# First two input projections accumulated tile by tile beside the modulation, and the steps of all stages placed one by one

## The chip, the cores and the metric

The kernel runs on one core of one Trainium2 chip. The metric is device time in microseconds (us); the median of three runs of the kernel before is 1701.49. TensorE is called PE here, VectorE DVE, ScalarE ACT, GpSimd POOL and SyncE SP, as in the profile. SP issues the transfers (DMAs); PE's results land in PSUM, from where DVE and ACT fetch them.

## The reference

One inference step of a transformer layer, on a batch of 1024 prompt frames and 64 sample frames, width D = 1024, all in fp32:

```python
mod = silu(c) @ w_ada + b_ada                       # 6 x 1024 shifts, scales, gates
h = rms_norm(x, norm1_g) * (1 + sc1) + sh1
proj = h @ w_in                                     # 3336 columns
...                                                 # columns 0-1791: RWKV-7 heads (8 x 64)
z = p_rwkv + (prev - p_rwkv) * shift_mu
r, k, v, dw, da, dg = split(z)
y_rwkv, s_new = rwkv_scan(...)                      # s = s*w + sa (kk a) + v k, y = s r
...                                                 # the rest: forgetting attention (8 x 64)
y_fox = softmax(q k^T / 8 + forget bias, causal) @ v
x = x + gt1 * (concat(y_rwkv, y_fox) @ w_out)
h2 = rms_norm(x, norm2_g) * (1 + sc2) + sh2
x = x + gt2 * ((silu(h2 @ w_ffn_gate) * (h2 @ w_ffn_up)) @ w_ffn_down)
```

Beside the output the step returns the RWKV state, the shifted row, and keys, values and log forget values.

## The kernel before

**Numbers.** Every large product is made of three matmuls: operands are split in a high part in a rounded format and a low part that holds the rest (`split_w`, L285: the cast whi on ACT, L212, the subtraction wlo on DVE, L216), and hi x hi, hi x lo and lo x hi are summed in PSUM (`mm3`, L291; lines L294, L295, L296). A weight tile of w_in is 1024 x 128 numbers, 512 KB; whi and wlo each have two buffers. One projection of a half of the tokens is 8 feature tiles x 3 = 24 matmuls.

**Tokens** go in two halves: half 0 has 512 columns, half 1 has 512 and the 64 sample frames, in two chunks of 288. Functions write the steps down in an order, a scheduler turns this into the order of the instructions on each engine.

**Start.** Modulation tile t of w_ada (16 of 48 are made here, in the order shift 0, scale 0, shift 1, scale 1, ...) takes 8 matmuls of 32x128 (`ada_mm`, L181, tile pada; the trace counts 16 records), a copy of the row by ACT (mrow, L193), a transpose on PE (L198) and on DVE a sum and an addition (mred, L200; mod, L201). After each pair DVE makes a gain (g, L204), and `h_part` makes feature tile k of the normed input: x on DVE (L270), its high part hhi on ACT (L271), its low part hlo on DVE (L272). SP loads the input, twelve modulation tiles, w_in tile 12, four modulation tiles, w_in tile 13. The splits of both come late, at tiles 12 and 15. Then come the projections of tiles 12 and 13 (for the low-rank gates), from PSUM buffers "mm".

**Phase.** Each half follows a string of steps (`ORDER`, L35; `phase`, L1286): Z (three projections k, r, v of one pair of RWKV heads), D, A, B, N (decay, triangular blocks, the recurrence, norm and output), Q, K, V (projections for the attention), q, k (norms), L, O, C, S, P (smaller steps). A round of modulation tiles left over (24, the "background") comes one ahead of each projection that loads a weight. Rows of B that the prediction speaks of: small 32x32 products pg (L523), one PSUM buffer for each head of the pair, tags rb and ch. What half 0 leaves undone is done later (T, U).

**Attentions.** Half 0 has 2 units per head, half 1 has 3, each of them in three parts: scores psc (L910, L912) with maximum and exponential, transposes ppt (L940) with splits pth and ptl, products with the values pav (L962). `Pipe(2)` runs each unit's first part two units ahead of its last. Between them half 1 has `residual_x`, `load_mix` (L984: tiles mixt of the mixed heads back from memory, split in mixrh, mixrl for the RWKV part, mixfh, mixfl for the attention part) and `outproj` of half 0 (matmuls po, 24 per output tile, O0 to O7), one output tile after each head. Between the two attentions PSUM buffers are laid out anew: first scores of half 1 need those of half 0 released.

**End.** Output projection of half 1, second norm, the feed-forward network and its down projection.

## Time and profile before

| | |
|---|---|
| median of three runs | 1701.49 us (1700.19 to 1702.09) |
| the profiled execution | 1699.15 us, its span 1697.5 us |
| ACT busy, DVE busy | 726.5 us (43%), 1124.8 us (66%) |
| bytes moved | 207.08 MB, mean 122 GB/s |
| mean granted clock of PE | 0.992 |

The profile covers one execution; times count from the span's start. A group's mean duration can mix shapes. PE's matmuls overlap in their records, so a matmul's cost in a row of them is the distance between two starts, not its duration. The granted clock is the share of full speed that PE was given.

### The profile page before, as it was taken

What the parts mean: (1) busy time and instruction counts of PE and PEld (TensorE: products, weight loads), DVE (VectorE), ACT (ScalarE), POOL (GpSimd) and SP (SyncE); (2) the same over time, 40 slices, a digit from 0 to 9 for tenths busy, and PEclk for the clock granted to TensorE, in tenths of its full rate; (3) what the DMA queues carried; (4) which work ended last, traced back from release to release, by engine and by line L of the source; (5) the groups of instructions that cost most, each with busy time, mean ns of one, the idle gap of its engine ahead of it and who ended that gap; (6) DMA issues with size and microseconds to landing.
All of it is one profiled execution on the core that took longest, in us unless ns stands there. A gap on an engine that the chain in (4) does not pass through costs nothing.

```text
span 1697.5 us, 33265 instructions
## 1 busy us (share of the span) xinstructions
PE 1645.3 (97%) x12897; PEld 1439.1 (85%) x12897; DVE 1124.8 (66%) x2573; ACT 726.5 (43%) x1530; POOL 183.1 (11%) x412
## 2 busy tenths in 40 slices
PE   6999999999999999989999999999999999999999
PEld 3776776788888888767889899999999999999998
DVE  6776676757867655877877975555555556545545
ACT  4535364653545346766776633333333333211210
POOL 2102230222121213201120000000000000000000
PEclk9999999999999999989999999999999999999999
DMA  8544447541233344566654432222222215323313
GB/s 308 164 128 133 141 135 200 176 123 33 71 85 85 87 135 113 149 190 179 169 181 167 157 127 77 77 77 77 77 77 77 77 65 196 134 79 97 97 40 121
DMA packets 133580, 207.08 MB, mean 122 GB/s; under 512 B 62126, under 2 KB 70350, under 8 KB 133422
## 3 DMA queue, kind: packets, MB, share of 16 engines
q1 hardware_dynamic: 133422, 204.95, 39.5%
q8 instruction: 102, 1.67, 0.4%
q14 instruction: 56, 0.46, 0.1%
HBM read 157.65 MB, written 47.25 MB: 121 GB/s over the span
## 4 chain that ended last, share of the span: by engine, by line
PE 84%; DVE 6%; ACT 4%; DMA 3%; issue 2%; SPq 0%; POOL 0%; ACTq 0%; DVEq 0%; POOLq 0%
PE pd L1275 15%; PE pfe L1160 8%; PE pfc L1160 7%; PE pfa L1160 7%; PE pmm L294 5%; PE pmm L295 5%; PE pmm L296 5%; PE pfb L1160 4%; PE pbs L375 2%; PE pav L962 2%; PE po L294 2%; PE ppt L940 2%; PE po L296 2%; PE po L295 2%; PE pA L464 2%
## 5 line engine op out<-in xcount | busy, mean ns | idle before, releaser
L294 PE MATMUL pmm<-hhi,whi 128*128 128x288 f32 (+1 forms) x624 | 218.8, 351 | 2.3 <-ACT pb L317 1.4
L295 PE MATMUL pmm<-hlo,whi 128*128 128x288 f32 (+1 forms) x624 | 217.0, 348 | 0.0
L296 PE MATMUL pmm<-hhi,wlo 128*128 128x288 f32 (+1 forms) x624 | 215.2, 345 | 0.6 <-DVE wlo L216 0.6
L212 ACT CAST whi<-wraw 128x1024 fp32r<-128x1024 f32 (+2 forms) x116 | 99.2, 855 | 212.5 <-PE pd L1275 167.0
L1275 PE MATMUL pd<-ah,wlo 128*128 128x512 f32 (+1 forms) x528 | 173.5, 329 | 0.0
L1275 PE MATMUL pd<-al,whi 128*128 128x512 f32 (+1 forms) x528 | 173.3, 328 | 0.0
L1275 PE MATMUL pd<-ah,whi 128*128 128x512 f32 (+1 forms) x528 | 173.1, 328 | 0.0
L1279 DVE SCALAR_TENSOR_TENSOR x1t<-pd,mod,x1t 128x512 f32<-128x512 f32 x192 | 91.4, 498 | 111.5 <-PE pd L1275 111.0
L294 PEld LDWEIGHTS pmm<-hhi,whi 128*128 128x128 f32 x624 | 119.0, 191 | 14.1 <-ACT pb L317 2.0
L296 PEld LDWEIGHTS pmm<-hhi,wlo 128*128 128x128 f32 x624 | 118.7, 190 | 10.9 <-issue 1.7
L295 PEld LDWEIGHTS pmm<-hlo,whi 128*128 128x128 f32 x624 | 118.7, 190 | 9.9 <-issue 1.2
L216 DVE TENSOR_TENSOR wlo<-wraw,whi 128x1024 fp32r<-128x1024 f32 (+2 forms) x108 | 104.2, 965 | 18.8 <-ACT whi L212 18.3
L1275 PEld LDWEIGHTS pd<-al,whi 128*128 128x128 f32 x528 | 99.4, 188 | 7.7
L1275 PEld LDWEIGHTS pd<-ah,whi 128*128 128x128 f32 x528 | 99.3, 188 | 7.7
L1275 PEld LDWEIGHTS pd<-ah,wlo 128*128 128x128 f32 x528 | 99.3, 188 | 7.5
L1160 PE MATMUL pfc<-hh,hS 128*128 128x256 f32 (+1 forms) x352 | 101.6, 289 | 1.6 <-ACT hh L1062 1.6
L1160 PE MATMUL pfc<-hl,hS 128*128 128x256 f32 (+1 forms) x352 | 101.9, 289 | 0.0
L1160 PE MATMUL pfa<-hh,whi 128*128 128x256 f32 (+1 forms) x352 | 101.9, 290 | 0.0
L1160 PE MATMUL pfa<-hl,whi 128*128 128x256 f32 (+1 forms) x352 | 101.8, 289 | 0.0
L1160 PE MATMUL pfc<-hh,lS 128*128 128x256 f32 (+1 forms) x352 | 101.5, 288 | 0.0
L1160 PE MATMUL pfa<-hh,wlo 128*128 128x256 f32 (+1 forms) x352 | 101.4, 289 | 0.0
L604 POOL TENSOR_SCALAR sd<-sv,pc 64x64 f32<-64x64 f32 x136 | 76.3, 561 | 181.2 <-DVE sv L617 157.6
(361 smaller groups left out, 4383.5 us busy)
## 6 DMA issues: line engine op xcount, KB each, us to landing
wraw<-in_w_in_dram SPq DMA_DIRECT2D x52, 512.0 KB
wada<-in_w_ada_dram SPq DMA_DIRECT2D x48, 512.0 KB
as<-actscr SPq DMA_DIRECT2D x22, 544.0 KB
wraw<-in_w_gate_dram SPq DMA_DIRECT2D x22, 512.0 KB
wraw<-in_w_up_dram SPq DMA_DIRECT2D x22, 512.0 KB
wraw<-in_w_down_dram SPq DMA_DIRECT2D x40, 256.0 KB
wraw<-in_w_out_dram SPq DMA_DIRECT2D x16, 512.0 KB
actscr<-sg SPq DMA_DIRECT2D x22, 288.0 KB
```

The costliest lines, as they stand in the source:

```text
L212: nc.scalar.copy(hi, src)
L216: eng.tensor_tensor(lo, src, hi.bitcast(F32), op=ALU.subtract)
L294: nc.tensor.matmul(ps[0:M, 0:n], whi[:, k, 0:M], xhi[:, k, off:off + n], start=(k == 0), stop=False)
L295: nc.tensor.matmul(ps[0:M, 0:n], whi[:, k, 0:M], xlo[:, k, off:off + n], start=False, stop=False)
L296: nc.tensor.matmul(ps[0:M, 0:n], wlo[:, k, 0:M], xhi[:, k, off:off + n], start=False, stop=(k == kt - 1))
L375: nc.tensor.matmul(ps[:, 0:n], w, x[:, off:off + n], start=True, stop=True)
L464: nc.tensor.matmul(pa[h][:, i], kb[hp, c + i], rk[hp, c + i], start=True, stop=True)
L604: nc.gpsimd.tensor_scalar(sd[hsl[h]], sv[hsl[h], c, h], pc[hsl[h], c], None, op0=ALU.mult)
L940: nc.tensor.transpose(pt[0:rows, b - b0, t * P:t * P + qn], p[0:qn, pc:pc + rows], self.ident[0:qn, 0:qn])
L1160: nc.tensor.matmul(ps, l[:, k], r[:, s, k], start=(first and k == 0 and y == 0), stop=(k == 3 and y == 2), skip_group_check=True)
L1275: nc.tensor.matmul(ps[:, 0:n], w[:, i], x[:, t:t + n], start=(i == 0 and y == 0), stop=(i == len(fs) - 1 and y == 2))
L1279: nc.vector.scalar_tensor_tensor(dst, ps[:, so - off:so - off + l], self.mod[:, 40 + o, b:b + 1], dst, op0=ALU.mult, op1=ALU.add)
```

## The change

No instruction is added or taken away; orders change in three places.

**Start.** The raw loads of w_in tiles 12 and 13 move up, behind modulation tiles 2 and 4; both splits stand ahead of the first feature tile. Two PSUM buffers are opened as sums, and after each feature tile its six matmuls (three per projection) are written down; `proj` then hands out the finished sums.

**Phases.** Z becomes X (k), Y (r) and W (v), each a step of its own, G is a background modulation tile given in the order, and A, B and T are generators, run in 3 or in 12 to 14 steps ("B0*12" runs twelve).

**Attentions.** `Pipe` goes; a string `ATT` gives every part of each unit, as a unit's number (0 stands for unit 0, each mention runs its next part), H for a head's loads, M and N for `load_mix` of half 0 and 1, R for `residual_x`, O for an output tile.

```diff
-ORDER = ("Z0 D0 A0 D1 Z1 L Q0 B0 V0 N0 A1 C0 Z2 D2 q0 O A2 K0 k0 B1 K1 V2 Z3 D3 Q1 q1 V1 C1 A3 S k1 Q2 N1 q2 Q3 B2 N2 K2 k2 V3 K3 k3 C2 q3 C3",
+ORDER = ("W0 X0 G Y0 G D0 A0*2 G D1 G X1 G Y1 A0 G W1 L G Q0 B0*12 G V0 N0 A1*3 C0 G X2 G Y2 G W2 D2 q0 A2 O A2*2 G K0 "
+         "k0 B1*12 G K1 G V2 G X3 G Y3 G W3 D3 G Q1 q1 G V1 C1 A3*3 S k1 G Q2 N1 B2 q2 G Q3 B2*11 N2 G K2 k2 G V3 G K3 "
...
+       "M H0 0 1 0 R 2 1 0 H1 3 2 1 4 3 2 5 4 3 O0 H2 6 5 4 7 6 5 8 6 7 O1 H3 9 8 7 10 9 8 11 10 9 O2 H4 12 11 10 13 "
...
     def proj(self, hf, col, evac):
+        if self.begun:
+            evac(self.begun.pop(0), 0, hf.n)
+            return
         if self.pre:
             whi, wlo = self.pre.pop(0)
         else:
-            if self.background:
-                self.background.pop(0)()
             whi, wlo = self.load_w(self.A["w_in"][col // P], [P, KT, P])
...
+    def att_phase(self, hf, order, more):
+
+        units = {}
+        for t in order:
+            if t[0] == "H":
+                us = self.attend(int(t[1:]), hf)
+                units.update({int(t[1:]) * len(us) + i: u for i, u in enumerate(us)})
+            elif t.isdigit():
+                next(units[int(t)], None)
+            else:
+                more[t[0]](int(t[1:] or 0))
...
                 for t in range(16):
-                    if t == 12:
-                        w_in(12)
+                    if t in (2, 4):
+                        w_in(11 + t // 2)
                     raw.append(self.ada_load(tile(t), "ada"))
-                w_in(13)
                 rs = self.x_stat(x0)
                 part = self.ada_mm(0, raw[0], "ra")
+                ws = [self.split_w(r, [P, KT, P]) for r in w]
+                self.begun = [self.ps([P, 512], tag="mm", name="pmm") for _ in w]
...
                     with tc.issue_after(part[4].ins):
-                        if t in (12, 15):
-                            self.pre.append(self.split_w(w.pop(0), [P, KT, P]))
                         if t and t % 2 == 0:
-                            self.h_part(hf, t // 2 - 1, x0[:, t // 2 - 1], rs)
+                            k = t // 2 - 1
+                            self.h_part(hf, k, x0[:, k], rs)
+                            for i, (whi, wlo) in enumerate(ws):
+                                for y, (a, b) in enumerate(((whi, self.hhi), (whi, self.hlo), (wlo, self.hhi))):
+                                    nc.tensor.matmul(self.begun[i], a[:, k], b[:, k, 0:512], start=(k == 0 and y == 0),
+                                                     stop=(k == KT - 1 and y == 2))
```

Line numbers in rows of the kernel after are its own, 12 to 34 higher than those before (L202 is the modulation matmul, L210 its transpose, L306 to L308 the three matmuls of a projection, L1466 those of the first two).

PE at the start, before: the last modulation tile, both last transposes, and then the first projection.

```order
L190 MATMUL pada<-wada,ct 32x128 x8
L198 MATMUL pada<-ident,mrow 128x128 x2
L294 MATMUL pmm<-hhi,whi 128x512
L295 MATMUL pmm<-hlo,whi 128x512
L296 MATMUL pmm<-hhi,wlo 128x512
```

PE at the start, after: one turn, the matmuls of feature tile 3 inside modulation tile 11 (its eight matmuls are cut in 1 and 7) and the two transposes behind it.

```order
L1466 MATMUL pmm<-hhi,whi 128x512 x2
L202 MATMUL pada<-wada,ct 32x128
L1466 MATMUL pmm<-hlo,whi 128x512
L1466 MATMUL pmm<-hhi,wlo 128x512
L1466 MATMUL pmm<-hlo,whi 128x512
L1466 MATMUL pmm<-hhi,wlo 128x512
L202 MATMUL pada<-wada,ct 32x128 x7
L210 MATMUL pada<-ident,mrow 128x128
L202 MATMUL pada<-wada,ct 32x128 x8
L210 MATMUL pada<-ident,mrow 128x128
```

The projections' matmuls moved from behind all modulation into it, and both transposes stand behind the matmuls that read hlo.

DVE in one turn of the same place, before:

```order
L200 TENSOR_REDUCE mred<-pada 128x2
L201 TENSOR_SCALAR mod<-mred,vc 128x2
L272 SCALAR_TENSOR_TENSOR hlo<-x_189,mod,hhi 128x512
L200 TENSOR_REDUCE mred<-pada 128x2
L201 TENSOR_SCALAR mod<-mred,vc 128x2
L204 SCALAR_TENSOR_TENSOR g_161<-mod,vc 128x2
L270 SCALAR_TENSOR_TENSOR x_189<-x_189,g_161,xacc 128x512
```

DVE in one turn, after:

```order
L212 TENSOR_REDUCE mred<-pada 128x2
L213 TENSOR_SCALAR mod<-mred,vc 128x2
L212 TENSOR_REDUCE mred<-pada 128x2
L284 SCALAR_TENSOR_TENSOR hlo<-x_189,mod,hhi 128x512
L213 TENSOR_SCALAR mod<-mred,vc 128x2
L216 SCALAR_TENSOR_TENSOR g_161<-mod,vc 128x2
L282 SCALAR_TENSOR_TENSOR x_189<-x_189,g_161,xacc 128x512
```

The second sum (mred), which needs the second transpose, moved ahead of hlo.

PE in half 0 at step B2, before: behind a projection (its last row here is pbs) and a background tile come products of both heads, pg_3365 for one and pg_3364 for the other, and then the next projection.

```order
L375 MATMUL pbs<-gsq,bmean 128x512
L190 MATMUL pada<-wada,ct 32x128 x8
L523 MATMUL pg_3365<-gt,At 32x32 x7
L368 MATMUL plora<-z,wg 128x512
L198 MATMUL pada<-ident,mrow 128x128
L523 MATMUL pw_3401<-g_3363,inv_692 32x32 x8
L523 MATMUL pu_3421<-inv_692,g_3363 32x32 x16
L523 MATMUL pg_3364<-gt,At 32x32 x16
L294 MATMUL pmm<-hhi,whi 128x512
```

The same place after (pgt and pu_3479 are later products of the first head):

```order
L388 MATMUL pbs<-gsq,bmean 128x512
L202 MATMUL pada<-wada,ct 32x128 x8
L540 MATMUL pw_3401<-g_3363,inv_742 32x32 x8
L540 MATMUL pu_3421<-inv_742,g_3363 32x32 x3
L381 MATMUL plora<-z,wg 128x512
L210 MATMUL pada<-ident,mrow 128x128
L540 MATMUL pu_3421<-inv_742,g_3363 32x32 x13
L540 MATMUL pgt<-gt,At 32x32 x8
L567 MATMUL pu_3479<-inv_742,gt 32x32 x8
L306 MATMUL pmm<-hhi,whi 128x512
```

The pg of the first head stand ahead of all this now, and pg_3364 come behind the projection that begins in the last row.

PE at the seam of the attentions, before: the last products of half 0 and the first scores of half 1.

```order
L962 MATMUL pav<-pth,vsx_8034 128x256
L962 MATMUL pav<-ptl,vsx_8034 128x256
L910 MATMUL psc<-k1x_9559,qsx_9557 128x512
L912 MATMUL psc<-k2x_9560,q2x_9558 128x512
```

PE at the seam, after (mixrh_9540 and mixrl_9544 are half 0's mixed RWKV heads):

```order
L306 MATMUL po<-mixrh_9540,whi 128x512
L307 MATMUL po<-mixrl_9544,whi 128x512
L984 MATMUL pav<-pth,vsx_8034 128x256
L962 MATMUL ppt<-ident,p 128x128
L308 MATMUL po<-mixrh_9540,wlo 128x512
L984 MATMUL pav<-ptl,vsx_8034 128x256
L306 MATMUL po<-mixrh_9540,whi 128x512
L984 MATMUL pav<-pth,vsx_8034 128x256
L962 MATMUL ppt<-ident,p 128x128 x2
```

SP at the seam, after, where the first load of a mix tile stands among the last loads for half 0:

```order
L895 DMA q2x_9558<-qx 64x576
L1018 DMA mixt<-yscr_71 128x512
L668 DMA yscr_72<-y 128x576
L901 DMA vsx_8034<-vscr_110 128x512
L996 DMA yscr_71<-fy 128x512
L1018 DMA mixt<-yscr_71 128x512
```

Matmuls of O0 moved from the first head of half 1 into the drain of half 0, twelve of them ahead of the first score, and the mix loads moved ahead of a store and of the last head's values.

146 lines of the change are left out of this document (72 added, 74 removed), and 3 rows, old and new, of the table ATT.

## The prediction

> **What bounds the kernel now.** I read the page first, then busy time by stretches, then the chain of waits at the places where a stretch had idle TensorE. The page's engine row:
>
> ```profile
> PE 1645.3 (97%) x12897; PEld 1439.1 (85%) x12897; DVE 1124.8 (66%) x2573; ACT 726.5 (43%) x1530; POOL 183.1 (11%) x412
> ```
>
> PE is busy 1645.3 of a span of 1697.5 us, so 52.2 us are idle, and the change keeps every PE instruction. What an order can win is idle time, and time at half clock. The stretches (length, then busy time of PE, PEld, DVE, ACT, POOL, then granted clock, DMA share, GB/s):
>
> ```profile
> 18.00:31.40 13.40, 9.28 (x187) 5.52 (x186) 10.95 (x34) 5.02 (x15) 6.32 (x21) 1.00 1.03 409
> 31.40:38.20 6.80, 6.13 (x42) 4.00 (x43) 6.07 (x20) 4.52 (x9) 0.00 (x0) 0.50 0.72 230
> 665.00:738.00 73.00, 65.56 (x522) 50.61 (x521) 58.91 (x190) 53.54 (x166) 17.92 (x56) 0.98 0.55 160
> 738.00:741.40 3.40, 2.25 (x12) 1.53 (x12) 2.53 (x8) 2.32 (x7) 0.15 (x2) 1.00 0.75 283
> 741.40:755.00 13.60, 11.98 (x40) 8.99 (x39) 7.17 (x14) 5.70 (x12) 0.41 (x2) 0.50 0.71 207
> 755.00:769.30 14.30, 13.06 (x76) 10.06 (x77) 10.62 (x24) 9.79 (x23) 0.35 (x2) 1.00 0.42 130
> 804.00:892.00 88.00, 87.98 (x540) 72.02 (x540) 70.54 (x145) 63.75 (x141) 18.43 (x27) 1.00 0.58 169
> 985.00:1431.00 446.00, 445.69 (x3545) 445.45 (x3544) 269.48 (x515) 138.31 (x256) 0.00 (x0) 1.00 0.26 85
> ```
>
> The reader should see two things. From 804 on PE is as good as full (87.98 of 88, later 445.69 of 446), so what is saved or lost before 804 reaches the end undiminished. And the open places are the start, where the first norm is made, and the seam between the two attentions at 738 to 769, where 1.15 + 1.62 + 1.24 = 4.0 us are idle and 11.98 us of PE work ran at a clock of 0.50, which is 6.0 us more than at full clock.
>
> **The start, part by part.** Before, the norm's loop goes round once per feature tile on DVE and ACT. The chain of waits:
>
> ```profile
> 20.34 0.75 DVE hlo L272
> ...
> 24.62 0.77 DVE x L270
> 25.41 0.73 ACT hhi L271
> 26.16 0.75 DVE hlo L272
> ...
> 27.48 0.76 DVE x L270
> ...
> 34.21 1.22 DVE wlo L216
> ...
> 39.88 1.34 DVE hlo L272 x2
> ```
>
> One feature tile costs 27.48 - 24.62 = 2.86 us (0.57 of it mred, mod and g between hlo and the next x), the first hlo ends at 21.1 and the last at 41.2. PE meanwhile (start, duration, instruction):
>
> ```profile
> 26.59 0.65 PE L190 MATMUL pada<-wada,ct 128*32 128x128 f32 x16
> 27.17 0.33 PE L198 MATMUL pada<-ident,mrow 128*128 128x128 f32 x1
> ...
> 47.59 0.40 PE L295 MATMUL pmm<-hlo,whi 128*128 128x512 f32 x1
> 47.82 0.40 PE L296 MATMUL pmm<-hhi,wlo 128*128 128x512 f32 x1
> 48.15 0.65 PE L190 MATMUL pada<-wada,ct 128*32 128x128 f32 x16
> 49.15 0.50 PE L294 MATMUL pmm<-hhi,whi 128*128 128x512 f32 x1 [0.36 <-ACT pb L317]
> ```
>
> Projection matmuls follow each other at 47.82 - 47.59 = 0.23 us at full clock. A modulation tile takes 27.17 - 26.59 = 0.58. The two projections end at 48.1, 6.9 us behind the last hlo; only that tail can be won.
>
> After the change, four matmuls per feature tile need its hlo and stand in PE's order inside the next modulation tile; DVE in turn has the sums (mred) of both next modulation tiles ahead of hlo, and ACT both row copies ahead of hhi. That closes a loop that was open before. Its remaining prices:
>
> ```profile
> L193 ACT COPY mrow<-pada x14: 245/265/268, 18.0 to 35.1; 128x128 f32<-128x128 f32 x14
> ```
>
> ```profile
> 35.25 1.05 ACT L212 CAST whi<-wraw 128x1024 fp32r<-128x1024 f32 x1
> ```
>
> One turn: hlo to four matmuls 0.93, seven eighths of a modulation tile 0.51, handover about 0.1 (an estimate from the gaps of 0.02 to 0.1 in the chain), row copy 0.27, hhi 0.73, hlo 0.75, handovers 0.06: 3.35 us, against 2.86. The early weight splits come on top. The first low part (1.22 on DVE, starting once its 1.05 cast is over) delays the first feature tile by about 0.5: hlo ends at 21.6. The second split lies between tile 0 and tile 1: its cast (1.05, all but 0.3 of it beside hlo), its low part 1.22, one matmul 0.23, a transpose 0.33, mred, mod and g 0.57, x, hhi and hlo 2.3 give about 5.0 for that turn. The next takes about a microsecond more than the loop, 4.35, since there the transpose for g comes behind tile 1's matmuls too, and x after it. Then four turns of 3.35 (13.4). The last has no modulation in it: g, x, hhi and hlo are 2.65. Sum: 21.6 + 5.0 + 4.35 + 13.4 + 2.65 = 47.0 for the last hlo, 0.93 more for the last matmuls: 47.9, where before had 48.1.
>
> What is late next is the third projection. Its high part needs the first weight buffer, which now stays taken until the last feature tile, where before it came free some 24 matmuls earlier. So cast 1.05 and low part 1.22 stand open, from 47.3 on: its third matmul, which needs the low part, starts at about 49.6. Before that was 49.15 + 0.47 = 49.6. So 6.9 us of tail are won and given back, 5.8 by the slower loop and about 1 by the open split. The modulation tile that filled the gap at 48.15 now comes later, which costs up to its 0.58. And the half clock, granted from 31.4 to 38.2 when PE waited anyway, would now lengthen a turn by 0.93 + 0.51 = 1.4, for two turns 2.8. I take **+1.0**, between -1 (no such stretch, splits quicker) and +4 (half clock as before). The two weight loads, moved up ten and twelve places in SP's queue, hold the modulation tiles behind them back by one or two landings of 1.3 us (512 KB at 409 GB/s, the first stretch above); I put that at nothing, since a loop of 3.35 takes a tile only every 1.7 us, and it would cost those 2.6 if the loop came to wait for tiles.
>
> The loop rests on PE taking its matmuls in program order. [...] In the trace the projections' matmuls and the tile at 48.15 follow in the written order, and no row shows one that overtook; without that rule the loop would stay at 2.86 and the start would gain, as in the second rival below.
>
> **The place of the third RWKV step B2.** Before, PE waits there, and then runs slow:
>
> ```profile
> 276.30 0.69 PE L523 MATMUL pg<-gt,At 32*32 32x32 f32 x32 [1.40 <-DVE y L644]
> ```
>
> ```profile
> 277.00:280.60 3.60, 3.60 (x8) 2.46 (x9) 1.87 (x5) 1.64 (x2) 0.00 (x0) 0.53 0.71 196
> ```
>
> Its waiting products (pg of the second head) stood ahead of a projection; now that projection goes ahead and they come a projection later. That takes the wait of 1.40; the clock of 0.53 after it cost another 1.7. I take **-1.4**, from 0 (another step waits for the same PSUM) to -3.1 (clock too). The other moves in the two phases (X, Y, W for Z, G in their places, steps of A and B between) leave long stretches of PE's order as it was; I put them at 0, with 2 us to either side, a bit more than the one wait that a single place showed.
>
> **The seam of the attentions.** PE waits and works there as follows:
>
> ```profile
> 738.69 0.33 PE L940 MATMUL ppt<-ident,p 128*128 128x128 f32 x1 [1.02 <-DVE p L928]
> ...
> 744.68 0.80 PE L910 MATMUL psc<-k1x,qsx 128*128 128x512 f32 x1 [0.97 <-DVE fy L969]
> ```
>
> ```profile
> 729.80 0.35 SPq L646 DMA_DIRECT2D yscr<-y  x1
> ...
> 746.00 0.90 SPq L984 DMA_DIRECT2D mixt<-yscr  x2
> ```
>
> ```profile
> 768.51 3.78 DMA mixt<-yscr
> ```
>
> The last units of half 0 drain with nothing beside them, and the first mix tile is asked for only at 746.00. The change puts the first of these loads just ahead of the store that was issued at 729.80, 16 us earlier, starts the splits ahead of the drain and lets 12 of the 24 matmuls of O0 run inside it, the other 12 inside the first head. Those 12 are 12 x 0.23 = 2.8 us, against 1.15 + 1.62 = 2.8 us idle up to 755. I take -2.5 of it, and -0.5 of the 1.24 later. Of the 6.0 lost to the clock I take half, -3.0: the low clock began behind 2.25 busy of 3.40 (66%), and the drain will be fuller, but how full is enough no row tells; the ends are 0 and -6.0. Against this stands work moved forward:
>
> ```profile
> L216 DVE TENSOR_TENSOR mixrl<-mixt,mixrh x8: 664/710/748, 756.5 to 849.4; 128x512 fp32r<-128x512 f32 x4, 128x576 fp32r<-128x576 f32 x4
> ```
>
> Four such low parts (0.71 each, 2.8 us) go into half 0's attention, where DVE has 58.91 busy of 73 and PE waits 7.4. The cover is DVE's idle 14 us; where it fails it costs 2.8, and I take +1.0. Together **-5.0**, between -10 and +2. Half 0's units in a new order from head 4 on I put at 0, within the ends just given: PE's 7.4 us of waits in 665 to 738 are open to them, but the work on each engine is the same. O6 and O7 between the last units of half 1 win nothing: from 804 PE is full.
>
> [...]
>
> **The sum.** +1.0 - 1.4 - 5.0 = -5.4 us. The profiled execution took 1699.15 (span 1697.5 and 1.65 around it) and would take 1693.75. It lies 2.34 under the median of the three runs, 1701.49, so against that median I forecast 1696.1. About 0.2% (3.4 us) is what a measurement of this kernel can tell from no change; the forecast is -0.32%.
>
> **The rivals.** First, no change: the seam's gaps are the latency of a softmax that drains and another that starts, and O0's matmuls are merely taken from the heads behind. For it: O0 ran in a stretch with 1.24 idle only. Against it: from 804 PE is full, so work moved into idle time is gone from there. The seam is then worth -0.5 to -1.5, the sum about -1.5: 1700.
>
> Second, the early projections are really hidden: splits fall into idle DVE time (18 to 31.4 has 2.45 idle), and the loop stays near 2.9. Then the last hlo comes near 43.0 and the third projection's third matmul at 43.3 + 2.3 = 45.6, where it was 49.6: -4.0 in place of +1.0, and -10.4 with the rest: 1691. Against it: the order puts the transposes behind the hlo matmuls.
>
> Third, slower: at the seam SP's queue is in order, and the mix loads now stand in it ahead of the last head's value tile (vsx) and of the RWKV output's store. If such a load waits for its buffer or for a store, all behind it waits, the last head with it. Its price is one load (3.78) and its split (low part 0.71, high part about as much by estimate), 5.2, where the gain of 5.0 was; the sum becomes +1.0 - 1.4 + 5.2 = +4.8: 1706. It decides once the hold is over 3.8 us. For it: loads are asked for one at a time, each bound to a split on busy ACT and DVE. Against it: SP comes to these loads 16 us earlier than before.
>
> **How the numbers follow.** Forecast case 0.52 (own range -9.5 to -1), no change 0.22, hidden start 0.11, slower 0.15. Faster by over 0.2%: two thirds of the first (0.35), the third case (0.11), a little of no change (0.02): 0.48. Slower: 0.13 of the slower case, 0.04 from the tails of the first two: 0.17. Within 0.2%: the remaining 0.35. For 8 in 10 the range runs from -11.0 (the hidden start, or the seam's full -10 beside the other terms, 1690.5) to +3.5 (start at +4, seam at +1, 1705.0); outside lie most of the slower case and a twentieth below.
>
> **What would show it.** Right: the last hlo at 46 to 49 and the third projection's third matmul at 49 to 53; PE idle under 1.5 us from 738 to 755 (shifted), with po instructions between pav; no wait of 1.40 at pg of B2. Wrong: hlo every 2.9 us; a first score of half 1 that waits for a mix load; the same half clock for over 10 us behind a filled drain; or any new wait over 2 us between 62 and 665, which I put at nothing.

## The result, and the profile after

The change made the kernel slower: 1720.26 us (1715.74 to 1723.99, 4 runs) against 1701.72 (1700.19 to 1702.09), a ratio of 1.0118 [1.0105, 1.0132] (the ratios and their 95% intervals are the estimates on record, and can differ a little from the quotient of the medians). The forecast was 1696.1 in 1690.5 to 1705.0. The profiled execution took 1715.74 with a span of 1714.0; it is the fastest of the four and lies 16.6 over the profiled one of before. The page's engine row after (busy time, share, instructions):

```profile
PE 1655.0 (97%) x12897; PEld 1440.8 (84%) x12897; DVE 1130.0 (66%) x2573; ACT 728.5 (43%) x1530; POOL 185.7 (11%) x412
```

PE has the same 12897 instructions, 59.0 us idle in place of 52.2, and 9.7 us more busy. To find the places I asked of both traces when PE had done the same amount of work (its matmuls added up in program order, each at its shortest duration). After stands behind before by 5.3 us at 50 us, 8.1 at 250, 12.5 at 740, only 5.2 at 800, 15.6 at 840, and 16.6 from 900 to the end. The count leans on each shape's shortest duration, so single figures are good to a microsecond or two. So there are four stories: a start that costs 5, another 7 lost on the way to 740, a seam that wins 7, and a stretch from 800 to 840 that loses 10.

**The start.** PE in one turn of the norm's loop after (start, duration, instruction), with the last matmuls of the two projections and the third projection behind:

```profile
41.71 0.50 PE L1466 MATMUL pmm<-hlo,whi 128*128 128x512 f32 x1
...
42.84 0.64 PE L202 MATMUL pada<-wada,ct 128*32 128x128 f32 x14
43.41 0.33 PE L210 MATMUL pada<-ident,mrow 128*128 128x128 f32 x1
...
52.44 0.39 PE L1466 MATMUL pmm<-hhi,wlo 128*128 128x512 f32 x1
53.76 0.50 PE L306 MATMUL pmm<-hhi,whi 128*128 128x512 f32 x1 [0.93 <-ACT pb L330]
...
54.53 0.50 PE L308 MATMUL pmm<-hhi,wlo 128*128 128x512 f32 x1
```

The projections end at 52.8 where they ended at 48.2, and the third projection's third matmul starts at 54.53 where it started at 49.72. DVE, the first turn and a later one (a turn runs from one hlo to the next):

```profile
20.79 0.75 DVE L284 SCALAR_TENSOR_TENSOR hlo<-x,mod,hhi 128x512 fp32r<-128x512 f32 x1 [0.45 <-ACT hhi L283]
...
25.66 0.17 DVE L212 TENSOR_REDUCE mred<-pada 128x2 f32<-128x8 f32 x1 [2.71 <-PE pada L210]
...
27.86 0.75 DVE L284 SCALAR_TENSOR_TENSOR hlo<-x,mod,hhi 128x512 fp32r<-128x512 f32 x1
...
40.88 0.74 DVE L284 SCALAR_TENSOR_TENSOR hlo<-x,mod,hhi 128x512 fp32r<-128x512 f32 x1
...
43.78 0.17 DVE L212 TENSOR_REDUCE mred<-pada 128x2 f32<-128x8 f32 x1 [1.04 <-PE pada L210]
...
44.61 0.17 DVE L212 TENSOR_REDUCE mred<-pada 128x2 f32<-128x8 f32 x1 [0.40 <-PE pada L210]
44.69 0.74 DVE L284 SCALAR_TENSOR_TENSOR hlo<-x,mod,hhi 128x512 fp32r<-128x512 f32 x1
```

The loop closed as forecast: hlo is asked of ACT and DVE only after PE's transposes (both mred name PE's pada as what they waited for), and those stand behind the matmuls that read the last hlo; PE ran them in the written order, hlo's matmuls from 41.71, the rest of the modulation tile at 42.84, its transpose at 43.41. The steady turn is 44.69 - 40.88 = 3.81 us, the first is 7.07, and the last hlo ends at 51.6, where 47.0 was forecast. The first falls into half clock, as this stretch shows (length, busy PE, PEld, DVE, ACT, POOL, clock, DMA share, GB/s):

```profile
18.00:27.00 9.00, 6.99 (x59) 3.74 (x59) 5.41 (x14) 2.43 (x5) 1.33 (x2) 0.62 1.02 409
```

**B2 and the phases.** PE after, at the largest wait behind the start, at B2, and where the first scores of half 0 are made:

```profile
78.17 0.50 PE L306 MATMUL pmm<-hhi,whi 128*128 128x512 f32 x1 [2.01 <-DVE mred L212]
...
263.30 0.69 PE L540 MATMUL pg<-gt,At 32*32 32x32 f32 x32
...
285.13 0.69 PE L567 MATMUL pu<-inv,gt 32*32 32x32 f32 x16 [1.17 <-ACT gt L563]
...
680.12 0.22 PE L938 MATMUL psc<-cmask,identb 128*128 128x128 bf16 x1 [1.16 <-DVE cmask L871]
```

The wait of 1.40 at pg is gone; one of 1.17 at pu has taken its place. Yet it is not the new order of the phases that took it: the kernels with the new phases and before's start (phases alone, all but the start) still have it, 1.40 at pg ahead of the projection, at 277.50 and 276.57. It is gone only where the start is new as well. The wait of 2.01 at 78.17, which a modulation tile's sum (mred) ended, is longer than any that before has behind its start (1.44 at most), and one of 1.67 at 176.40 is new too. Another, 1.16, stands where a unit's mask (cmask) is not ready. The ones at pu and at the mask are followed by half clock:

```profile
285.00:290.00 5.00, 4.87 (x26) 3.26 (x27) 0.65 (x3) 2.36 (x5) 0.28 (x1) 0.66 0.76 195
681.00:689.00 8.00, 8.00 (x59) 6.34 (x57) 6.07 (x20) 5.05 (x17) 2.48 (x6) 0.57 0.30 103
```

The 8 us at a clock of 0.57 cost, by estimate, 8.00 x 0.43 = 3.4 (the time, times the share of the clock that is missing). Before ran at 0.50 at this place too, from 673.10 to 676.50, though with PE busy for 3.25 of the 3.40 us ahead, so 1.7 of the 3.4 is new.

**The seam and what follows it.** PE at the seam, before and then after, over about the same work:

```profile
728.00:795.00 67.00, 59.92 (x312) 45.16 (x313) 49.13 (x107) 40.48 (x95) 5.34 (x19) 0.90 0.65 184
```

```profile
740.00:800.20 60.20, 52.75 (x283) 40.55 (x284) 42.10 (x95) 35.90 (x83) 4.78 (x15) 0.94 0.72 202
```

The 7 us won here are not idle time: PE idles 7.1 us before and 7.5 after. They are busy time. Half of it is clock: before ran at half clock (0.50) for 13.6 us from 741.4, after (0.50 as well) for 6.8 from 767.3, which by the same estimate is 3.4 us. The rest no row here splits.

Output matmuls (po) alone, before, in stretches of 15 us (length, busy PE with count, clock, DMA share, GB/s):

```profile
765.00:780.00 15.00, 7.78 (x24) 1.00 0.77 211
780.00:795.00 15.00, 4.19 (x14) 1.00 0.56 134
795.00:810.00 15.00, 3.42 (x11) 1.00 0.57 147
810.00:825.00 15.00, 5.42 (x17) 1.00 0.71 181
825.00:840.00 15.00, 7.12 (x24) 1.00 0.62 187
```

The same view after:

```profile
765.00:780.00 15.00, 6.17 (x17) 0.77 0.95 255
780.00:795.00 15.00, 6.88 (x23) 1.00 0.61 154
795.00:810.00 15.00, 4.88 (x15) 1.00 0.40 103
810.00:825.00 15.00, 0.00 (x0) 1.00 0.44 104
825.00:840.00 15.00, 0.00 (x0) 0.96 0.72 182
```

Before, O0 to O3 are spread over the heads; after, O0 to O2 are used up by 810, and for 30 us the attention's heads have no output matmul to fill their waits. PE as a whole there, after; from 804 to 892 before had it 87.98 of 88 busy:

```profile
800.00:848.00 48.00, 42.46 (x255) 33.48 (x253) 37.95 (x78) 32.41 (x74) 6.53 (x14) 0.96 0.47 125
836.00:848.00 12.00, 10.92 (x54) 8.61 (x54) 8.07 (x18) 6.61 (x16) 1.19 (x3) 0.86 0.33 100
```

5.5 of 48 us are idle, and the last row runs at 0.86. What the next output tile lacks is its weight. SP's queue after, then before (start, duration, DMA):

```profile
824.92 0.45 SPq L899 DMA_DIRECT2D vsx<-vscr  x1
825.42 0.58 SPq L294 DMA_DIRECT2D wraw<-in_w_out_dram  x1
```

```profile
811.24 0.45 SPq L877 DMA_DIRECT2D vsx<-vscr  x1
811.74 0.58 SPq L282 DMA_DIRECT2D wraw<-in_w_out_dram  x1
```

In both, the weight of O3 is asked for right behind a head's value tile (vsx). That load goes out late in both, so O3 starts late in both, at 826.1 before and 843.4 after, however early O2 is done.

### The profile page after: what moved, and what is told of

It is laid out like the page before. It is cut to its first block, busy times and chain, and to the rows that moved or that the text cites. A ratio compares the mean times of both kernels' runs of the same rounds, so it can differ in the third digit from the quotient of the medians.

```text
span 1714.0 us, 33268 instructions
## 1 busy us (share of the span) xinstructions
PE 1655.0 (97%) x12897; PEld 1440.8 (84%) x12897; DVE 1130.0 (66%) x2573; ACT 728.5 (43%) x1530; POOL 185.7 (11%) x412
## 3 DMA queue, kind: packets, MB, share of 16 engines
q8 instruction: 102, 1.67, 0.4%
## 4 chain that ended last, share of the span: by engine, by line
PE 85%; DVE 6%; ACT 4%; DMA 3%; issue 2%; POOL 0%; SPq 0%; ACTq 0%; DVEq 0%
PE pd L1309 15%; PE pfc L1194 8%; PE pfe L1194 8%; PE pfa L1194 8%; PE pmm L306 5%; PE pmm L307 5%; PE pmm L308 5%; PE pfb L1194 4%; PE pav L984 2%; PE pbs L388 2%; PE po L306 2%; PE ppt L962 2%; PE po L308 2%; PE po L307 2%; PE pA L478 2%
## 5 line engine op out<-in xcount | busy, mean ns | idle before, releaser
L306 PE MATMUL pmm<-hhi,whi 128*128 128x288 f32 (+1 forms) x608 | 211.9, 349 | 3.3 <-DVE mred L212 2.0
L308 PE MATMUL pmm<-hhi,wlo 128*128 128x288 f32 (+1 forms) x608 | 210.1, 346 | 0.3 <-DVE wlo L228 0.3
L307 PE MATMUL pmm<-hlo,whi 128*128 128x288 f32 (+1 forms) x608 | 208.1, 342 | 0.0
L306 PEld LDWEIGHTS pmm<-hhi,whi 128*128 128x128 f32 x608 | 115.2, 190 | 15.9 <-issue 2.5
L308 PEld LDWEIGHTS pmm<-hhi,wlo 128*128 128x128 f32 x608 | 115.5, 190 | 9.8 <-issue 1.2
L228 DVE TENSOR_TENSOR wlo<-wraw,whi 128x1024 fp32r<-128x1024 f32 (+2 forms) x108 | 103.8, 961 | 28.4 <-ACT whi L224 27.7
```

What stands on the lines that cost most here:

```text
L228: eng.tensor_tensor(lo, src, hi.bitcast(F32), op=ALU.subtract)
L306: nc.tensor.matmul(ps[0:M, 0:n], whi[:, k, 0:M], xhi[:, k, off:off + n], start=(k == 0), stop=False)
L307: nc.tensor.matmul(ps[0:M, 0:n], whi[:, k, 0:M], xlo[:, k, off:off + n], start=False, stop=False)
L308: nc.tensor.matmul(ps[0:M, 0:n], wlo[:, k, 0:M], xhi[:, k, off:off + n], start=False, stop=(k == kt - 1))
```

## The experiments

Four theories stood against each other. A: the parts cost on their own and add up (start, phases, seam). B: the late start is swallowed by the phases behind it, and all loss is at the seam and in the phases. Loop: the start costs because hlo's matmuls stand ahead of the transposes in PE's order. S (formed after the first four runs): output tiles run ahead, then O3's weight is late and the heads run bare; asking for weights early mends it. All kernels compute the whole reference. They ran on five chips; before took 1700.17, 1700.62, 1699.61, 1700.31 and 1699.23 on them, and each time stands beside before's on the same chip, with the ratio to it.

**Parts alone.** The start alone (`ORDER` and `ATT` write out the order of before, with the modulation tiles in their old places):

```diff
-ORDER = ("W0 X0 G Y0 G D0 A0*2 G D1 G X1 G Y1 A0 G W1 ...
+ORDER = ("G X0 G Y0 G W0 D0 A0*3 D1 G X1 G Y1 G W1 ...
-         "X0 Y0 T3 W0 T3*11 L D0 ...
+         "X0 Y0 W0 T3*12 L D0 ...
-ATT = (... "M H0 0 1 0 R 2 1 0 H1 ... 7 O1 ... O7 22 O6 23 22 23")
+ATT = (... "H0 0 1 0 2 1 0 R M H1 ... 6 O1 ... 23 O7")
```

> Only the new start; phases and attentions as before. Theory A (the three parts add): in the trace of the kernel after, PE reaches the same work 6.5 us later from 80 us on, and nothing later gives it back, so 1701.7 + 5 to 7 = 1707 to 1709. Rival B (a late start is swallowed by waits of the phases, which are idle 14 us anyway): 1702 to 1704.

1721.56 (1713.39 to 1727.74), 1.0124 [1.0098, 1.0151]: as dear as the whole change. Not swallowed, so B falls. But this kernel is not the start alone in what the engines run. The steps behind the start are written as before, yet the scheduler laid them out anew: compared by operand names and shapes, of the 1977 PE instructions that before has from 60 to 300 us, at most 1508 stand in the same order here, and of the 3117 from 300 to 650 at most 2564. In B0 of half 0, for instance, before has seven projection matmuls between two groups of pg (183.83 to 185.34), here there are none (185.01 to 188.59). The kernel with the pure delay, below, has all 1977 and all 3117 in before's order. The clock falls in these new stretches, three times for over 10 us where before has full clock (201.1, 467.3 and 617.5); the second and the 3.4 us ahead of it:

```profile
463.90:467.30 3.40, 3.40 (x60) 2.63 (x55) 2.15 (x6) 0.00 (x0) 0.00 (x0) 1.00 0.05 8
467.30:481.00 13.70, 13.70 (x224) 12.64 (x224) 3.64 (x8) 5.83 (x13) 3.38 (x7) 0.50 0.20 51
```

By its record PE did not wait there at all; most of these matmuls are small products of B (32x32 and 64x128). The profiled run took 28.4 more than before's. The third projection's third matmul starts at 54.85, 5.1 late, and the mean clock of 0.978 against 0.992 is worth, by estimate, (1725.9 x 0.022 x 2 - 1697.5 x 0.008 x 2) / 2 = 24.4: together 29.5.

The phases alone (before's start and `ATT`, new `ORDER`):

> Only the new strings of the phases; start and attentions as before. Theory A: the lag of the kernel after grows by 2.7 us from 100 to 650, so 1703 to 1706. Rival B (that growth is a clock stretch that the late start shifted): 1700 to 1702. My prediction had 0 with 2 to either side and -1.4 for step B2: 1698 to 1702.

1705.30, 1.0034 [1.0019, 1.0049]. The wait of the mask is there too, at its own place in this kernel:

```profile
671.82 0.22 PE L930 MATMUL psc<-cmask,identb 128*128 128x128 bf16 x1 [1.17 <-DVE cmask L863]
```

One of 1.15 at 883.18 is new as well, with 3.4 us of half clock behind it. Its 12 runs spread from 1699.46 at a mean clock of 0.997 to 1712.72 at 0.986. The attentions alone (before's start and `ORDER`, new `ATT`):

> Only the new order of both attentions; start and phases as before. Theory A: +3 in half 0's attention, -7 at the seam, +10 where two heads have no output-projection matmuls beside them, +1 behind: 1701.7 + 7 = 1707 to 1710. Rival B (the stretch without these matmuls comes of the lag that the start and the phases bring): the seam's gain stays, 1695 to 1699.

1708.61, 1.0051 [1.0030, 1.0071]. By the count of PE work it stands 7.2 ahead of before at 800, and 3.2 behind at 840. Its output matmuls stop as in the whole change:

```profile
795.00:810.00 15.00, 1.93 (x6) 1.00 0.57 147
810.00:825.00 15.00, 0.00 (x0) 1.00 0.70 180
825.00:840.00 15.00, 6.18 (x21) 0.89 0.55 168
```

All but the start (both new strings, before's start):

> The kernel after with the start of before. Theory A: 1720.3 - 6.5 = 1713 to 1715. Rival B: within 2 us of the kernel after, 1718 to 1722.

1711.61, 1.0074 [1.0053, 1.0094]. The two parts give 5.1 + 8.4 = 13.5 apart and 11.4 together. Against the whole (18.5 over its own before, on another chip) the start is worth some 7 in this company, and 21 beside the old phases: the parts do not add, but each of them costs.

**The start taken apart.** In the whole change, the six matmuls of a feature tile written one tile later, so that the transposes for the next tile no longer stand behind them:

```diff
-for i, (whi, wlo) in enumerate(ws):
+for q in ((k - 1,) if k < KT - 1 else (k - 1, k)):
+    if q < 0:
+        continue
+    for i, (whi, wlo) in enumerate(ws):
...
```

> The kernel after, but the six matmuls of a feature tile are written down one feature tile later, so that none of them needs the hlo made last. Theory L (the turn of 3.8 us is the loop hlo, matmuls, modulation tile, row copy, hhi, hlo): the turn falls to 2.9 to 3.1, the last hlo ends at 44 to 46 in place of 51.6, and the third projection begins 4 to 6 us earlier than in the kernel after (53.8). The time: 1713 to 1717 if that reaches the end. Rival (the turn is what the early splits and PE's load of matmuls cost, whatever their order): turn 3.6 to 3.8, no change in the time, 1718 to 1722.

1742.57 (1723.17 to 1746.88), 1.0224 [1.0183, 1.0265]. The turns of hlo became 5.5, 5.4, 3.4, 3.9, 3.1, 4.0 and 2.4, and the third projection's third matmul came at 52.20, 2.3 earlier than after: opening the loop gives back half of the direct delay, though the turn did not fall to the 2.9 to 3.1 that was expected. The kernel still became the slowest of all. Its profiled run of 1746.88 (span 1745.2) had a mean clock of 0.974: if all that is missing is half clock (0.50, as in the rows above), an estimate of 1745.2 x (1 - 0.974) x 2 = 91 us at half clock, where before, at 0.992, has 1697.5 x 0.008 x 2 = 27. Much of it lies far behind the start. One long stretch of this kernel, and then the same of before:

```profile
300.00:700.00 400.00, 388.21 (x3433) 329.32 (x3426) 256.31 (x696) 188.06 (x440) 86.13 (x175) 0.93 0.35 96
```

```profile
300.00:700.00 400.00, 388.72 (x3616) 330.93 (x3616) 279.17 (x779) 207.60 (x507) 96.50 (x202) 1.00 0.37 101
```

PE is as busy and does 183 matmuls fewer. Here too the order is another: at most 1574 of the 1977 and 2522 of the 3117 are in before's. Now the loads and splits early, but the matmuls behind the whole norm as before:

```diff
-self.begun = [self.ps([P, 512], tag="mm", name="pmm") for _ in w]
+self.pre = ws
...
-for i, (whi, wlo) in enumerate(ws):
-    ...
```

> The kernel after with the raw loads and splits early, but the matmuls of both projections behind the whole norm again. Theory L: turn 2.9, last hlo at 42 to 43, the two projections end at 47.5 to 48.5 as before, 1711 to 1714, as without the new start (1711.6). Rival (the early splits are what costs): last hlo later than 44, 1716 or more.

1729.49 (1722.35 to 1734.35), 1.0163 [1.0139, 1.0188], with the third projection's third matmul at 51.68. The turns are back at 2.9 from the third on (25.04, 28.03, 30.89), and the last hlo ends at 42.9, as the loop theory has it: without the matmuls in the loop there is no slower turn. The clock was 0.978. So moving the loads and splits alone delays the start by 2.0, and the matmuls in the loop by 2.9 more (54.53). But the time of the kernel does not follow these delays: it stands 28.9 over its own before, the kernel without the new start (1711.61) 11.4. A pure delay of the start, 14 multiplications by 1.0 on DVE ahead of the first feature tile, in before:

```diff
+for _ in range(14):
+    nc.vector.tensor_scalar(rs, rs, 1.0, None, op0=ALU.mult)
```

> The kernel before with 14 multiplications by 1.0 of the norm's 128x512 row factors on DVE ahead of the first feature tile, PE's and SP's order unchanged: a delay of about 5 us and nothing else. Theory A (a late start is carried to the end, no more): 1704 to 1706 at the same mean clock as before. Rival C (a delay alone brings new half-clock stretches later on, as in the runs with new starts): 1708 or more, at a mean clock under 0.988.

The third matmul starts at 51.45, 1.7 late instead of the 5 that were meant, and the time is 1700.50, 1.0006 [0.9997, 1.0015]. The interval, -0.5 to +2.6 us, holds nothing as well as the whole 1.7, so the run does not tell whether a delay is carried to the end. It does tell that a late start alone brings no loss of 20 us, as long as all that follows keeps its order. What is dear goes with the new order behind the start; the three kernels in which it strays furthest from before's (the start alone, and the two before this one: at most 2520 to 2564 of 3117, all others 2944 or more) are also the three with the lowest clock in their profiled runs: 0.978, 0.974 and 0.978, where all others have 0.985 or more. No run changes this order alone.

**The output tiles.** Weights of O3 to O7 asked for one head earlier, in the kernel with the new attentions alone:

```diff
- ... O0 H2 ... O1 H3 ... O2 H4 ... O3 H5 ... O4 N H6 ...
+ ... O0 W3 H2 ... O1 W4 H3 ... O2 W5 H4 ... O3 W6 H5 ... O4 W7 N H6 ...
+ "W": lambda j: self.prew.update({j: self.raw_w(A["w_out"][j], [P, KT, P])}),
```

> Old start and phases, new attentions, but the raw weights of O3 to O7 are asked for one head earlier. Theory S (the 10 us behind 800 are two heads without output-projection matmuls, since SP comes to O3's weights only then): the matmuls of O3 start ahead of the fifth head's scores, the lag stays at about -7 behind the seam, 1694 to 1699. Rival (heads 3 and 4 are held by DVE and ACT, whatever PE has beside them): O3 earlier, but the heads keep their times, 1705 to 1709 as in the run with the attentions alone.

1709.61, 1.0057 [1.0041, 1.0073]: no gain. The gap had only moved forward: O1 ended at 780, and O2 began only at 815.7, since its own weight, by the written order now the fifth, went out only at 800.39. Its output matmuls:

```profile
780.00:795.00 15.00, 0.41 (x2) 1.00 0.69 173
795.00:810.00 15.00, 0.00 (x0) 1.00 0.61 173
```

The same kernel with the mix loads back behind head 0's first units:

```diff
- M H0 0 1 0 R 2 1 0 H1 ...
+ H0 0 1 0 2 1 0 R M H1 ...
```

> Old start and phases, new attentions, but the mix loads of half 0 stand behind head 0's units as before. Theory S: no matmuls of O0 in the drain, so no gain at the seam (lag 0 to -1 there), and since O0 to O2 don't run ahead, only part of the gap behind 800 opens (there is a head without output matmuls in its order between the third and the fourth): 1701 to 1707. Rival (the gap comes from the units' new order): 1709 or more, the gap's 10 us without the seam's gain.

1706.84, 1.0038 [1.0024, 1.0053]: the interval overlaps that of the attentions alone, so the early mix loads are not the whole cost, and the new order of units costs without them. The early mix loads alone, in before's order of units:

```diff
- H0 0 1 0 2 1 0 R M H1 ...
+ M H0 0 1 0 2 1 0 R H1 ...
```

> The kernel before with one move: the mix loads of half 0 stand ahead of head 0's loads. Theory S (output matmuls that run ahead must last until the weights of O3 come): the seam gains 6 to 7 as in the kernel after, and the order leaves a little more than one head without output matmuls between O2 and O3, so half of it is lost again: 1696 to 1700. Rival H (the heads keep the pace of DVE and ACT whatever PE does, so matmuls that ran ahead win nothing): 1701 to 1705.

1710.21, 1.0057 [1.0041, 1.0074], above both forecasts. PE work is 3.8 ahead at 800 and 12.9 behind at the end: the seam wins and the stretch behind takes it back. The same with the first four weights ahead of the mix loads and the others behind the tiles:

```diff
- M H0 0 1 0 2 1 0 R H1 ... O0 H2 ... O1 H3 ... O2 H4 ... O3 H5 ...
+ W0 W1 W2 W3 M H0 0 1 0 2 1 0 R H1 ... O0 W4 H2 ... O1 W5 H3 ... O2 W6 H4 ... O3 W7 H5 ...
```

> As the run with the mix loads first, and the raw weights of O0 to O3 are asked for ahead of head 0, those of O4 to O7 four output tiles ahead, so that the order has output matmuls beside every head. Theory S: the seam's gain stays, 1693 to 1697. Rival H: 1701 to 1705.

1704.03, 1.0018 [1.0007, 1.0030]: 6.2 won. The direction is that of S, but the time is the one that its rival H had (1701 to 1705), not the 1693 to 1697 of S. The profiled runs took 1700.15 at a clock of 0.993, and 1711.95 at 0.988 without the early weights; by estimate 0.005 x 1700 = 8.5 of these 11.8 is clock, so the direct gain is smaller. Half 0's new order of units alone:

```diff
- H4 8 7 6 9 8 7 H5 10 9 8 11 10 9 ... H7 14 13 12 15 14 13 15 14 15
+ H4 8 7 9 8 6 7 H5 10 9 9 8 11 10 ... H7 13 12 14 15 13 14 14 15 15
```

> The kernel before with the new order of units in half 0's attention only; half 1's part as before. If the lag of about 3 that the kernel after gains from 650 to 740 comes of this order: 1702 to 1705. Rival (it came of the clock there): 1699 to 1702. In the order this kernel has no output matmuls between O2 and the fifth head, so by theory S a loss of about 2 to 5 behind 800 as well; by rival H none.

1705.26, 1.0034 [1.0021, 1.0046]: I had this at 0; it costs 5.7. Half 1 is written as before here, and still its order on PE is another: of the 818 instructions from 760 to 900 in before, at most 696 are in the same order. It is, instruction by instruction, the order that the kernel with the phases alone has there. Both have a wait that before has not, with 3.4 us of half clock behind it, by estimate 1.2 + 1.7 = 2.9 us together:

```profile
882.48 0.38 PE L976 MATMUL pav<-ptl,vsx 128*128 128x256 f32 x1 [1.16 <-DVE ptl L968]
```

Both new attention strings with the weights first:

> The new attentions (old start and phases), with the raw weights of O0 to O3 ahead of head 0 and the others four output tiles ahead. Its order has output matmuls beside every head. Theory S: the 10 us behind 800 are gone but for the new unit order's few, 1698 to 1702. Rival H: as with the attentions alone, 1706 to 1710.

1698.98 (1697.17 to 1702.73, 11 runs), 0.9999 [0.9990, 1.0008]: the 8.4 of the attentions alone are gone. The output matmuls no longer stop:

```profile
795.00:810.00 15.00, 4.76 (x14) 1.00 0.70 182
810.00:825.00 15.00, 7.38 (x22) 1.00 0.70 174
```

and the weight of O3, the fourth in SP's order, which went out at 811.74 in before, now goes at

```profile
705.33 0.36 SPq L286 DMA_DIRECT2D wraw<-in_w_out_dram  x1
```

It equals before, and is no better: 5.3 us ahead at 800 in PE work, it is 0.7 behind at the end all the same. Half 0 old, half 1 new with weights first:

> Start, phases and half 0's attention as before; half 1's attention in the new order with the raw weights of the output projection asked for early. If the parts add (new attentions with early weights 1699.0, of which half 0's new order costs 3 to 5.6), 1694 to 1697, the fastest so far. Rival: half 0's units and half 1's seam belong together, and this one is at 1698 to 1702.

1705.15, 1.0028 [1.0015, 1.0041]. That is 0.3% worse than with half 0's new units beside it, although those cost 5.7 when alone. These terms do not add. An edit in one place changes the order in others too, so the kernels of this section are not clean sums of parts.

**In company.** The whole change with the weights first:

> The whole change, with the raw weights of the output projection asked for early. Theory S: the 10 us behind 800 go, all else of the kernel after stays: 1709 to 1712. Rival (with the start's and the phases' lag the heads need them later anyway): 1716 to 1722.

1726.79, 1.0162 [1.0145, 1.0179]. The change again on another chip, and two more of its parts beside it:

> The whole change as it is, on one chip with the two kernels below, so that the parts can be set against it run for run. From the first runs: 1717 to 1723, at a mean clock of 0.986 to 0.990.

1724.70, 1.0143 [1.0130, 1.0157]: 25.5 over its before, where it was 18.5 in the first runs, so differences between chips are good to some 7 us only. The change without the new start, weights first:

> Phases and attentions new, start as before, the raw output weights asked for early. Without early weights this was 1711.6. If the missing output matmuls are the loss also beside the new phases: 1702 to 1706. If early weights help only beside the old phases (as the whole change with early weights, at 1726.8, suggests): 1709 to 1714.

1711.81, 1.0075 [1.0060, 1.0090], equal to the 1711.61 without the early weights. The start and phases without the new attentions:

> Start and phases new, attentions as before. If the parts add, start 6.5 direct and phases 5: 1711 to 1714. If the new start brings half-clock stretches in all that follows: 1716 or more at a mean clock under 0.988.

1715.46 (1711.30 to 1726.91), 1.0096 [1.0070, 1.0123]. So on one chip, by the medians (the six runs here spread widely): the new attentions add 1724.70 - 1715.46 = 9.2 to start and phases, as they add 8.4 to before. Beside the new phases early weights win nothing. In the kernel without the new start they did bring the output matmuls back; PE waits at another place instead, in a stretch where DVE is 13.05 of 15 busy:

```profile
795.00:810.00 15.00, 11.98 (x66) 9.19 (x67) 13.05 (x24) 10.16 (x23) 3.07 (x5) 0.90 0.27 80
```

```profile
802.53 0.44 PE L954 MATMUL ppt<-ident,p 128*128 128x128 f32 x2 [1.40 <-DVE p L942]
```

S is thus shown for the seam beside the old phases (new attentions from 8.4 to -0.6, mix loads first from 10.6 to 4.4), and is not the cause that decides in the whole change.

## Why the prediction was wrong

**The steps that failed** are two. By the count of PE work the miss is 16.6 + 5.4 = 22.0 us in the profiled run; 4.3 of it are the start (5.3 by 50 us, where +1.0 was forecast), 8.6 come by 740 (7.2, where -1.4 was), 8.1 by 840 (+3.1, where -5.0 was), and 1.0 later.

The first is "The other moves in the two phases ... leave long stretches of PE's order as it was; I put them at 0"; nor did the start's +1.0 count anything behind the start. The order did not stay: of before's 1977 PE instructions from 60 to 300 us at most 1693 stand in the same order after, and of the 3117 from 300 to 650 at most 2944. The scheduler answers an edit at one place with other orders behind it, and new waits (2.01, 1.67, 1.17, 1.16) and half clock come with them.

The second is "from 804 on PE is as good as full ..., so what is saved or lost before 804 reaches the end undiminished". PE was full there because O0 to O7 lay evenly between the heads. The forecast took twelve of their matmuls away from that place and went on counting the place as full. In before's order O2's second half and the first of O3 stand between the scores of heads 3 and 4; in after's, no output matmul stands between O2's end and head 4's scores. That could be read before the run, as could SP's row at 811.74: O3's weight is bound behind a head's value tile, so O3 cannot follow O2 forward. That this gap costs the time is shown beside the old phases; beside the new ones early weights do not bring it back.

**The seam**, put at -5.0: 7.3 were won between 740 and 800 by the count of PE work, with po inside the drain from 750.86, but not as forecast. The idle time, put at -3.0, stayed (7.1 and 7.5); half clock, put at -3.0, gave 3.4. Then 10.4 were lost between 800 and 840. The attentions alone cost 8.4 where -5.0 was forecast, and give it back once the weights are early.

**The start**, put at +1.0: the mechanism was right, its size was not. Turns of 3.35 were 3.81: ahead of hlo there is one more wait, DVE's second mred, 0.40 behind PE, and the matmuls behind hlo took 42.84 - 41.71 = 1.13, not 0.93. The turn of 5.0 took 7.07 at a clock of 0.62; the forecast had the half clock among its bounds (2.8) but not in its value. Of the 4.6 by which the last hlo was late, 2.1 are this first turn, 0.9 the second (5.22 for 4.35) and 1.9 the four behind it (15.35 for 13.4), less 0.3 in the last. The third projection's third matmul was forecast at 49.6 and came at 54.53. The direct delay, 54.53 against 49.72, is 4.8, above the upper end of +4. The whole cost is larger still: 12.9 beside the other parts on one chip (1724.70 against 1711.81, the latter with early weights), 7 across chips (18.5 - 11.4), and 21 alone. What goes beyond the direct delay is, by the estimate above, mostly clock in the start alone (24.4 of 28.4 in its profiled run).

**B2**, put at -1.4: the wait went, but by luck, for beside before's start the new phases leave it where it was; and one of 1.17 at pu took its place, so next to nothing was won. **The other moves in the phases**, put at 0 with 2 us to either side: the phases alone cost 5.1. The one wait at the mask that seven of the nine profiled runs with the new phases show (1.16 or 1.17; the kernels with the matmuls a tile later and with the loads and splits early lack it) makes, by estimate, 1.2 + 1.7 = 2.9 of it in the profiled run, since before ran 3.4 us at half clock there too; the one at 883.18, with its half clock, makes as much again.

**Half 0's units**, put at 0: +5.7 alone, of which some 2.9 fall in half 1, whose order changed with them.

**The rivals.** The first rival named the mechanism of the second failed step, O0's matmuls taken from the heads behind; it was set aside with the sentence that failed, and its own 1700 was far too low. The slower case was the right sign by another mechanism: no head waited for a mix load. With the attentions alone, head 0's last score came at 754 as in before. The hidden start falls with turns of 3.81 and a first one of 7.07.

**The signs.** Of those for being right, po stood between pav, and the wait of 1.40 went, though not through the phases; the last hlo (51.6, not 46 to 49), the third matmul (54.53, not 49 to 53) and PE's idle time at the seam (2.8 us from 738 to 755 in before, 2.9 from 750 to 767 after, not under 1.5) missed. Of those for being wrong, a new wait over 2 us came, 2.01 at 78.17; another profile of the same kernel has one of 3.25, at 256.82.

**What stays open.** With the start alone, the mean clock of its runs was 0.978 to 0.989, with the matmuls a tile later 0.972 to 0.988, where before had 0.988 to 0.997 and 0.989 to 0.998 beside them; the time went with it (the start alone from 1713.39 at 0.989 to 1727.74 at 0.979). The first 55 us reach hundreds of microseconds further through the order of what follows; that this order lowers the clock is likely from the three kernels named above, but no run changes it alone. Nor is it settled how the loss of the whole change divides over its new waits, why the terms of the two attentions do not add, or why early weights do not help beside the new phases; there I have the wait at ppt and a clock of 0.90, in one kernel. No version ran faster than before by more than the noise.

## To carry to other kernels

When a filler (here the output matmuls) is moved forward into a gap, ask what filled the place that it leaves, and whether the next filler can follow; a stretch that is full is full because of what you are about to take. When an operation is closed into a loop with another engine, add every wait in the ring at the clock that this stretch is granted, not at full clock (here the first turn, at 0.62, took 7.07 us where 5.0 was forecast). Where a scheduler lays out the order, an edit at one place can change the order everywhere behind it: compare the whole order of the engine that bounds the kernel before calling a stage unchanged, in a forecast and in an experiment with one part alone.

## What the runs showed of the hardware

**The clock.** At 0.50 products pav started every 0.21 to 0.22 us (742.23 to 743.30 in before), at 1.00 every 0.12 (833.28 to 834.47 after). Half clock came behind waits of 1.16 to 1.17 us: at 680.12 after, PE was busy for 2.24 of 3.40 us up to 682.00, and the clock was 0.50 until 688.80; at 285.13, 2.23 of 3.40 up to 286.60, and 0.59 until 290.00. The wait of 1.40 ahead of 276.30 in before had it too (2.00 of 3.40 busy up to 277.30, then 0.50 until 280.50). The longest wait of PE after behind its start, 2.01 ahead of 78.17, had none: 1.65 of 3.40 busy up to 77.90, then 1.00 until 86. And it came with no such wait, behind 3.25 of 3.40 busy in before (673.10, above), and behind 3.4 us in which PE's record has no gap (3.40 busy of 3.40 from 463.90 in the start alone, then 13.7 us at 0.50); the matmuls there were mostly small. So neither the length of a wait nor PE's busy share tells in these rows when half clock comes. A run's time went with its mean clock in the kernel with the phases alone: its twelve runs spread over 13 us for 0.011 of mean clock, from 1699.46 at 0.997 to 1712.72 at 0.986, more than most edits here are worth. A median over many runs is needed for such a verdict. The mean clock alone doesn't give the time either: a run of the attentions alone took 1713.16 at 0.938, another 1709.54 at 0.990.

**DVE and POOL beside each other.** The same operation on DVE, and what POOL did then (both after):

```profile
821.56 0.61 DVE L950 TENSOR_SCALAR p<-p,ls 128x768 f32<-128x768 f32 x1
...
834.11 2.59 DVE L950 TENSOR_SCALAR p<-p,ls 128x640 f32<-128x640 f32 x1
```

```profile
833.98 2.36 POOL L228 TENSOR_TENSOR wlo<-wraw,whi 128x1024 fp32r<-128x1024 f32 x1
```

A smaller tile took 2.59 beside POOL's split of O3's late weight; the other four of this form in this run, with no split beside them, took 0.54 to 0.56. In before the same form took 1.85 at 877.61, beside a split of 2.40 from 876.72, and 0.55 to 0.56 with none beside it. What holds DVE up there no run shows. Here the split ptl that PE waits for, at 836.62, stands behind the scaled p of 834.11 in DVE's order; the longest wait of PE between 800 and 848 follows.

```profile
837.08 0.38 PE L984 MATMUL pav<-ptl,vsx 128*128 128x256 f32 x1 [1.87 <-DVE ptl L976]
```
